# A hybrid encoder layer on one core: fewer, larger transfers for bias, reciprocals and v, and the modulation's gate by columns

## The chip, the cores and the metric

The kernel runs on one core of a Trainium2 chip. Its time is device microseconds of one execution. Five engines work side by side: TensorE (PE) multiplies matrices, VectorE (DVE), ScalarE (ACT) and GpSimd (POOL) do elementwise work, and SyncE (SP) issues nearly all transfers between DRAM and on-chip memory. The transfers themselves run on the core's 16 DMA engines.

## The reference

A layer over 512 tokens of 1024 channels, in float32: a modulated norm, one wide projection, a recurrent branch (A), a windowed attention branch (B), and a gated merge.

```python
mod = silu(c) @ w_c + b_c                     # 3 * 1024 columns
shift, scl, gate = split(mod, 3)
h = rms_norm(x, g_pre) * (1 + scl) + shift
xa, za, q, k, v, zb, ga, gb = split(h @ w_in, 8)      # each 512 x 1024
xa  = depthwise_conv(xa)
y_a = (rg_lru(xa, forward) + rg_lru(xa, backward)) * silu(za) @ w_pa
y_b = neighbourhood_attention(q, k, v, rpb) * silu(zb) @ w_pb
merged = sigmoid(ga) * y_a + sigmoid(gb) * y_b
x = rms_norm(x + gate * (merged @ w_o), g_final)
```

The tokens are a grid of 8 rows and 64 columns. The attention has 16 heads of 64; each query sees all 8 rows and 16 columns around its own, and a bias table rpb is added to the scores.

## The kernel before

Each matrix product is made of three: operands are split into a high part (rounded to the engine's fp32r) and a low remainder, and high x high, high x low and low x high are added. So a weight tile wraw (128 x 1024, 512 KB) is loaded by SP, cast by ACT into whi, and subtracted by POOL or DVE into wlo; then 24 matmuls of 128 x 512 use it. That is one `proj`, a projection of 128 output channels for all tokens.

The stages, in the order of the program:

1. The head: x and the modulation's weights arrive; shift and scale are made as columns (one value to a partition) by a multiply-and-add over rows (`modulate`); h is made tile by tile, and with each tile of h TensorE adds to the eight tiles of v (`vmm`). There are dummy matmuls in the first microseconds (`fill`).
2. v leaves through `vout`: ACT and DVE split a tile of v (128 tokens x 512 channels) into va, and SP writes it to a scratch tensor in DRAM (vscr0 for the first four pairs of heads, vscr1 for the others), eight writes of 512 KB.
3. The attention works on four groups of two pairs of heads. For each pair there are three projections (q, k, z), numbered by `main` from 9 on: 9, 10, 11 for pair 0, 12, 13, 14 for pair 1. Then `scores` multiplies q and k for both pairs, and `attend` does softmax and the product with v, while TensorE goes on with the next group's projections between its pieces. The rows of v are reloaded from vscr by `load_v`, in column-major order of the grid, as pieces vt. `bias` loads the bias braw, and POOL makes the masked tables nb. The reciprocals of the softmax's sums go through a DVE transpose, a 16 KB write to rscr with the access pattern `turned` and a reload as rcx that repeats them over 64 partitions; DVE then multiplies z's gate sz by rcx.
4. The recurrent branch, its gates, and the products with w_pb.
5. The merge: projections with w_pa, and `gate_row`, which makes the modulation's gate as a row: 16 loads wr of w_c, 16 multiply-adds on DVE (g), a split, four matmuls with ones (mi) that repeat the row over partitions, and the bias on top.
6. The product with w_o, whose rows are multiplied by the gate first, and the final norm.

The order on every engine is set ahead by a planner (`Plan`): an operation has a rank, dependencies and an estimated cost, and is placed on its engine when the estimate lets it begin. Large tiles come from NW slots of 128 x 1024, small ones from NS slots of 128 x 512. The engines then run their lists in order, and wait for what a row needs. SP's transfers take turns on eight counters (DMAHW0 to DMAHW7): a transfer waits until the one eight before it has landed.

A load's access patterns are written outermost dimension first. These are the ones of the transfers that the change and the prediction name, in the program before:

```python
src = bass.AP(rpb.tensor, ..., [[RPB_C, ROWS], [1, 16], [1, 256]])               # braw: 8 x 16 x 256 in DRAM
src = vscr[n].ap[g].rearrange("(r c) n -> c r n", r=ROWS)[c0:c0 + n // 8]        # vt: 16 (or 8) x 8 x 512
dst = vscr[n].ap[:, t * P:(t + 1) * P, :].rearrange("g p c -> p g c")            # vscr: 128 x 2 x 512
return bass.AP(scr.tensor, scr.offset, [[32, 4], [P, 32], [1, 32]])              # rscr: 4 x 32 x 32
src = bass.AP(scr.ap.tensor, ..., [[0, 64], [2 * P, 4], [1, P]])                 # rcx: 64 x 4 x 128, twice
```

The on-chip side is 128 partitions, 64 for rcx and for the half pieces of vt.

Of the kernel before, what the change touches and what calls it, by code (L numbers as in the profile page):

```python
# [8 lines left out]
F32 = mybir.dt.float32  # L9
# [20 lines left out]
NS, NW = 36, 32  # L30
# [3 lines left out]
QP, QE, BD = 1, 1, 0  # L34
LIMITS = {"hx": 8, "acc": 3, "sp": 8, "pt": 2, "pv": 2, "mi": 2, "hd": 3, "gt": 8}
# [297 lines left out]
def layer(ctx, tc, x, x_t, par, w_m, w_g, bc_gate, w_v, w_in, w_blk, rpb, amask, w_pa, w_pb, w_o, g_final, out):  # L333
# [64 lines left out]
    ident, onesc, onesr = const("ident", [P, P]), const("onesc", [P, P]), const("onesr", [P, P], F32R)  # L398
    prm, silc, msk, par_sb = const("prm", [P, 120]), const("silc", [P, KD]), const("msk", [P, 80]), const("par_sb", [120, P])
# [13 lines left out]
    op("PE", 0.25, lambda e: nc.tensor.transpose(pp0.ap[:, :120], par_sb.ap, ident.ap[:120, :120]), -20,  # L413
       r=[par_sb, ident], w=[pp0])
    op("DVE", 0.3, lambda e: nc.vector.tensor_copy(prm.ap, pp0.ap[:, :120]), -20, r=[pp0], w=[prm])
# [14 lines left out]
    for n in range(2):  # L430
        cb = B("hx")

        def f(e, n=n, cb=cb):
            for k in range(4):
                nc.tensor.matmul(cb.ap[:, k * P:(k + 1) * P], ident.ap[:120, 4 * n + k:4 * n + k + 1].to_broadcast([120, P]), par_sb.ap,
                                 start=True, stop=True)
# [96 lines left out]
    def modulate(k):  # L533

        for m, d in ((1, scs), (0, shs)):
# [24 lines left out]
            load(t, whole(t), w_m[2 * k + m], k - 5, 524288, spare=2, name=f"wc{k}{m}")  # L560
# [103 lines left out]
    vscr = [pl.fixed(dp.tile([2, S, 512], F32, name=f"vscr{n}")) for n in range(2)]  # L664

    def vout(u, rank):
        n, t = u
        a = W("va", F32R)

        def view(off, step):  # L670
            part = list(a.ap.ap)[0]
            return bass.AP(a.ap.tensor, a.ap.offset + off, [part, [256, 4], [step, 2], [1, 64]])
        src = lambda: vps[u].ap.rearrange("p (a b c) -> p a b c", a=4, b=2)
        op("ACT", act(512), lambda e: nc.scalar.copy(view(0, 192), src()), rank, r=[vps[u]], w=[a], name="voh")
        op("DVE", dve(512), lambda e: nc.vector.tensor_tensor(view(64, 64), src(), view(0, 192).bitcast(F32), op=ALU.subtract),
           rank, r=[vps[u]], rw=[a], name="vol")
        dst = vscr[n].ap[:, t * P:(t + 1) * P, :].rearrange("g p c -> p g c")
        op("SP", 0.6, lambda e: nc.sync.dma_start(dst, a.ap.bitcast(F32).rearrange("p (g c) -> p g c", g=2)), rank - 3,
           r=[a], w=[vscr[n]], size=524288, name="vout")
# [43 lines left out]
    def bias(pr, rank, after):  # L723
        raw = T("braw")
        rv = lambda: raw.ap.rearrange("p (h f) -> p h f", h=2)
        base = RPB_L - 1 - (PAD + 2 * pr * RPB_N + RPB_C * (ROWS - 1) + 7 + 255)
        for h in range(2):
            src = bass.AP(rpb.tensor, rpb.offset + base - h * RPB_N, [[RPB_C, ROWS], [1, 16], [1, 256]])
            load(raw, lambda h=h: rv()[:, h, :], src, rank - 4, 131072, after=after, spare=4, name="bias")
        res = []  # L730
        for v0, w, m0 in ((0, 32, 0), (8, 24, 32), (0, 24, 56)):
            nb = T("nb")
            res.append(nb)
            for h in range(2):
                def f(e, h=h, nb=nb, v0=v0, w=w, m0=m0):
                    part = list(raw.ap.ap)[0]
                    mv = msk.ap[:, m0:m0 + w].unsqueeze(1).to_broadcast([P, ROWS, w])
                    view = bass.AP(raw.ap.tensor, raw.ap.offset + h * 256 + 255 - v0, [part, [-RPB_C, ROWS], [-1, w]])
                    o = nb.ap.rearrange("p (h f) -> p h f", h=2)[:, h, :ROWS * w].rearrange("p (r c) -> p r c", c=w)
                    nc.gpsimd.tensor_tensor(o, mv, view, op=ALU.subtract)  # L740
                op("POOL", pool_(ROWS * w), f, rank - 1, r=[raw, msk], w=[nb], after=after, spare=2, name="nb")
        return res
# [7 lines left out]
    def load_v(g, after):  # L750
        for b in (0, 3, 1, 2):
            for j, (c0, r0) in enumerate(PIECES[b]):

                a = vt[g, b, j] = T("vt", F32R)
                n = 64 if (b, j) in ((0, 1), (3, 0)) else P
                src = vscr[g // 2].ap[g % 2].rearrange("(r c) n -> c r n", r=ROWS)[c0:c0 + n // 8]
                load(a, lambda a=a, r0=r0, n=n: a.ap[r0:r0 + n, :].bitcast(F32), src, 8 + 6 * g - 1.5 + 0.1 * (b > 0), n * 2048,
                     r=[vscr[g // 2]], after=after, spare=3, name="vt")
                if n == 64:
                    op("POOL", 0.7, lambda e, a=a, r0=r0: nc.gpsimd.memset(a.ap[64 - r0:P - r0, :].bitcast(F32), 0.0), 8 + 6 * g - 1.5,  # L760
                       w=[a], after=after, spare=3, name="vz")
# [42 lines left out]
    def attend(pr, sps, z, nbt, pos, pos0):  # L804
# [3 lines left out]
        def half(bs):  # L808
# [10 lines left out]
            for members in groups:  # L819
# [12 lines left out]
                for i, (b, h) in enumerate(members):  # L832
                    def f(e_, i=i, b=b, h=h, pv2=pv2):
                        c = 2 * bs.index(b) + h
                        nc.scalar.activation(pv2(i), pv2(i), AF.Exp, bias=mn.ap[:, c:c + 1], scale=-1.0,  # L835
                                             accum_out=sm.ap[:, 2 * b + h:2 * b + h + 1])
# [17 lines left out]
                def f(e_, members=members, ppv=ppv):  # L854
                    for i, (b, h) in enumerate(members):
                        e = bs.index(b)
                        for j in range(2):
                            mm(pv[h].ap[:, e * 256:(e + 1) * 256], vt[pr // 2, b, j].ap[:, off + h * P:off + (h + 1) * P],
                               ppv()[:, (i if edge else 2 * i) + j].rearrange("p s q -> p (s q)"), j == 0, j == 1)
                op("PE", 0.49, f, rk - 0.4, r=[pp] + [vt[pr // 2, b, j] for b in dict(members) for j in range(2)],  # L860
# [46 lines left out]
    def small(rank, after):  # L907
# [4 lines left out]
        op("DVE", 0.2, lambda e: nc.vector.tensor_scalar(silc.ap, pc(0, 8), 0.5, None, op0=ALU.mult), rank, r=[prm], w=[silc])  # L912
# [24 lines left out]
    for g in range(4):  # L937
        sets, zs, nbs = [], [], []
        for pr in (2 * g, 2 * g + 1):
            n0 = len(main)  # L940
            nbs.append(bias(pr, n0 + BD * (1 - pr % 2), gate_of(n0, 2) if pr else [main[6]]))
            if pr % 2 == 0:
                load_v(pr // 2, gate_of(n0, 2) if pr else [])
# [3 lines left out]
            sets.append(split(q, k))  # L947
        pos = k[0] + 0.6 + QP
        for i, sps in enumerate(scores(sets, pos, ends[-1:] if QE else [])):
            attend(2 * g + i, sps, zs[i], nbs[i], pos + 3 * i, pos)  # L950

# [141 lines left out]
    def gate_row(pos, after):  # L1093
        op("ACT", 0.3, lambda e: nc.scalar.copy(onesr.ap, onesc.ap), pos, r=[onesc], w=[onesr], after=after)
        g = (T("g"), T("g"))
        for kk in range(KD):
            for n in range(2):
                wr = T("wr")
                load(wr, whole(wr), w_g[kk * P:(kk + 1) * P, n * 512:(n + 1) * 512], pos + 0.5 * kk, 262144,
                     after=after, spare=12, name="wr")  # L1100

                def f(e, kk=kk, n=n, wr=wr):
                    if kk == 0:
                        nc.vector.tensor_scalar(g[n].ap, wr.ap, silc.ap[:, 0:1], None, op0=ALU.mult)
                    else:
                        nc.vector.scalar_tensor_tensor(g[n].ap, wr.ap, silc.ap[:, kk:kk + 1], g[n].ap, op0=ALU.mult, op1=ALU.add)
                op("DVE", dve(512), f, pos + 3 + 0.5 * kk, r=[wr, silc], **({"rw": [g[n]]} if kk else {"w": [g[n]]}), lock=True,
                   name="grow")
        for n in range(2):
            gh, gl = T("gh", F32R), T("gl", F32R)  # L1110
            op("ACT", act(512), cast(whole(gh), whole(g[n])), pos + 8, r=[g[n]], w=[gh])
            op("DVE", dve(512), sub(whole(gl), whole(g[n]), whole(gh)), pos + 8, r=[g[n], gh], w=[gl], lock=True)
            o, bcg, gf = B("mi"), T("gate"), T("gfin")

            def f(e, gh=gh, gl=gl, o=o):
                mm(o.ap, onesr.ap, gh.ap, True, False)
                mm(o.ap, onesr.ap, gl.ap, False, True)
            op("PE", 0.46, f, pos + 8, r=[onesr, gh, gl], w=[o], name="grow")
            load(bcg, whole(bcg), bc_gate[n * 512:(n + 1) * 512].partition_broadcast(P), pos + 7, 262144, after=after, spare=8)

            def f(e, o=o, bcg=bcg):
                nc.vector.tensor_tensor(bcg.ap, o.ap, bcg.ap, op=ALU.add)

                nc.vector.tensor_scalar(bcg.ap, bcg.ap, 0.5, None, op0=ALU.mult)
            op("DVE", dve(512) + dve2(512), f, pos + 8.2, r=[o], rw=[bcg], lock=True, name="gate")
# [203 lines left out]
```

## Time and profile before

| | |
|---|---|
| median of 3 runs | 561.11 us (560.77 to 564.41) |
| profiled execution, its own time | 561.85 us |
| its span, first to last instruction | 560.1 us |
| granted TensorE clock | 0.996 |
| TensorE busy | 550.8 us |
| DVE, ACT, POOL busy | 392.7, 322.1, 99.0 us |
| moved by DMA | 83.58 MB, 36509 packets |

The page gives busy times by engine, then 40 slices of the span, the DMA queues, the chain of work that ended last, the costliest groups of instructions and the transfers. Queue q1 is SP's, q10 ACT's. A row of a timeline has the start and the duration in us; a row of a group has busy time, the mean of one in ns, and the idle time ahead of it with what ended it. A row of windows begins with the stretch, then has busy time for PE, PEld, DVE, ACT and POOL, the granted clock, the mean busy share of the 16 DMA engines, and GB/s.

### The profile page before, as it was taken

The page shows a single profiled execution, that of the slowest core. Times are in us where ns is not written, and L with a number is a line of the kernel's source. Part 1 is how long each engine was busy: PE and PEld are TensorE (multiplying, and loading weights), DVE is VectorE, ACT ScalarE, POOL GpSimd, SP SyncE. Part 2 cuts the span into 40 slices and gives each one's busy share as a digit, 9 for nine tenths or more (in the row PEclk, how much of TensorE's full clock was granted, in tenths as well). Part 3 has the DMA queues.
Part 4 walks back from the last instruction along what each step waited for, and adds up shares of the span by engine and source line. Part 5 has one row for each costly group of instructions (what it writes and reads, how often), then busy time and mean ns, then how long its engine had stood idle before and what let it go on. Part 6 is the DMA issues. An engine that isn't in the chain of part 4 may idle for free.

```text
span 560.1 us, 7705 instructions
## 1 busy us (share of the span) xinstructions
PE 550.8 (98%) x2773; PEld 458.0 (82%) x2773; DVE 392.7 (70%) x712; ACT 322.1 (58%) x560; POOL 99.0 (18%) x97
## 2 busy tenths in 40 slices
PE   8999999999999999999999999999999999999995
PEld 8888888788888888887887888888788888888885
DVE  5998723684884886897569648866967897469523
ACT  6542523862763763777965984995698243223243
POOL 1102539453553540000000000000000000000220
PEclk9999999999999999999999999999999999999998
DMA  8993899439249244034333134032319452380002
GB/s 302 409 407 109 308 272 286 128 109 235 66 120 248 59 135 149 2 97 151 112 113 95 39 112 142 28 114 75 114 59 361 144 188 75 130 321 1 0 39 113
DMA packets 36509, 83.58 MB, mean 149 GB/s; under 512 B 4607, under 2 KB 11895, under 8 KB 36471
## 3 DMA queue, kind: packets, MB, share of 16 engines
q1 hardware_dynamic: 36192, 82.76, 45.2%
q8 instruction: 22, 0.36, 0.3%
q10 hardware_dynamic: 279, 0.32, 0.2%
q14 instruction: 16, 0.13, 0.1%
HBM read 76.65 MB, written 6.42 MB: 148 GB/s over the span
## 4 chain that ended last, share of the span: by engine, by line
PE 96%; DMA 2%; DVE 0%; SPq 0%; ACT 0%; POOL 0%; issue 0%; POOLq 0%
PE acc L384 78%; PE hx L384 8%; PE pv L384 3%; PE pt L842 2%; PE gt L384 2%; PE sp L384 2%; DMA wv<-in_w_v_dram 1%; DMA xT<-in_x_t_dram 1%; SPq L373 0%; POOL vl L381 0%; PE mi L384 0%; DVE yo L1216 0%; ACT vh L378 0%; DVE pp L850 0%; ACT pp L848 0%
## 5 line engine op out<-in xcount | busy, mean ns | idle before, releaser
L384 PE MATMUL acc<-hhl,whi 128*128 128x512 f32 x784 | 244.7, 393 | 0.0
L384 PEld LDWEIGHTS acc<-hhl,whi 128*128 128x128 f32 x784 | 143.7, 188 | 27.6 <-issue 0.4
L384 PE MATMUL acc<-hhl,wlo 128*128 128x512 f32 x392 | 152.9, 390 | 0.0
L384 PEld LDWEIGHTS acc<-hhl,wlo 128*128 128x128 f32 x392 | 73.6, 188 | 15.8
L378 ACT CAST whi<-wraw 128x1024 fp32r<-128x1024 f32 x72 | 74.2, 1044 | 9.1 <-DMA wraw<-in_w_in_dram 8.5
L1195 POOL TENSOR_TENSOR yo<-yo,gfin 128x512 f32<-128x512 f32 x6 | 8.0, 1339 | 338.0 <-ACT xr L1192 337.9
L381 POOL TENSOR_TENSOR wlo<-wraw,whi 128x1024 fp32r<-128x1024 f32 x23 | 56.1, 2444 | 63.6 <-ACT whi L378 49.4
L381 DVE TENSOR_TENSOR wlo<-wraw,whi 128x1024 fp32r<-128x1024 f32 x49 | 59.4, 1220 | 8.2 <-ACT whi L378 8.0
L384 PE MATMUL acc<-woh,mhl 128*128 128x512 f32 (+1 forms) x144 | 40.4, 365 | 0.0
L384 PE MATMUL acc<-yahl,whi 128*128 128x512 f32 x128 | 39.4, 389 | 0.0
L384 PE MATMUL acc<-ybhl,whi 128*128 128x512 f32 x128 | 39.4, 389 | 0.0
L740 POOL TENSOR_TENSOR nb<-msk,braw 128x192 f32<-128x192 f32 (+1 forms) x48 | 27.7, 610 | 35.6 <-DMA braw<-in_rpb_dram 29.4
L835 ACT ACTIVATE p<-p,mn 128x192 f32<-128x192 f32 (+1 forms) x64 | 30.5, 478 | 5.9 <-DVE mn L828 5.8
L384 PE MATMUL hx<-vh,hhl 128*128 128x512 f32 x112 | 33.5, 389 | 0.0
L828 DVE CUSTOM_DVE_ANT_0 p<-sp,nb 128x192 f32<-128x192 f32 (+1 forms) x64 | 31.6, 608 | 0.9 <-PE sp L384 0.7
L1070 DVE SCALAR_TENSOR_TENSOR gm<-gm,acc 128x512 f32<-128x512 f32 x16 | 11.0, 687 | 28.6 <-PE acc L384 28.5
L384 PEld LDWEIGHTS acc<-woh,mhl 128*128 128x128 f32 x144 | 26.1, 189 | 4.4
L384 PEld LDWEIGHTS acc<-yahl,whi 128*128 128x128 f32 x128 | 24.0, 188 | 5.0
L384 PEld LDWEIGHTS acc<-ybhl,whi 128*128 128x128 f32 x128 | 24.0, 188 | 5.0
L976 DVE SCALAR_TENSOR_TENSOR xc<-acc,prm,xc 128x511 f32<-128x511 f32 (+1 forms) x24 | 18.0, 749 | 12.3 <-ACT xc L969 11.7
L850 DVE TENSOR_TENSOR pp<-pt,pp 128x384 fp32r<-128x384 f32 (+1 forms) x32 | 19.5, 625 | 10.1 <-ACT pp L848 9.8
L384 PE MATMUL acc<-wol,mhl 128*128 128x512 f32 (+1 forms) x72 | 26.3, 365 | 0.0
(202 smaller groups left out, 960.7 us busy)
## 6 DMA issues: line engine op xcount, KB each, us to landing
wraw<-in_w_in_dram SPq DMA_DIRECT2D x56, 512.0 KB, 5.6
wc<-in_w_m_dram SPq DMA_DIRECT2D x14, 512.0 KB, 9.1
vt<-vscr SPq DMA_DIRECT2D x24, 256.0 KB, 7.8
vscr<-va SPq DMA_DIRECT2D x8, 512.0 KB, 5.3
wraw<-in_w_pb_dram SPq DMA_DIRECT2D x8, 512.0 KB
wraw<-in_w_pa_dram SPq DMA_DIRECT2D x8, 512.0 KB, 7.6
wr<-in_w_g_dram SPq DMA_DIRECT2D x16, 256.0 KB, 3.9
wo<-in_w_o_dram SPq DMA_DIRECT2D x8, 512.0 KB, 3.7
```

Source lines behind the costliest of these rows:

```text
L378: return lambda e: nc.scalar.copy(o(), i()) if e == "ACT" else nc.vector.tensor_copy(o(), i())
L381: return lambda e: ENGINE[e].tensor_tensor(o(), a(), b().bitcast(F32), op=ALU.subtract)
L384: nc.tensor.matmul(o, a, b, start=first, stop=last)
L740: nc.gpsimd.tensor_tensor(o, mv, view, op=ALU.subtract)
L828: nc.vector.tensor_tensor_reduce(out=o, in0=v(spv(h, e)[:, :nk]), in1=v(nb[:, h, :nk]), scale=1.0, scalar=3e38, op0=ALU.add, op1=ALU.min, ...
L835: nc.scalar.activation(pv2(i), pv2(i), AF.Exp, bias=mn.ap[:, c:c + 1], scale=-1.0, accum_out=sm.ap[:, 2 * b + h:2 * b + h + 1])
L842: nc.tensor.transpose(ptp.ap[:, j * P:(j + 1) * P], pt_.ap[:, j * P:(j + 1) * P], ident.ap)
L850: op("DVE", dve(nt * P), lambda e_, ppv=ppv, pv4=pv4: nc.vector.tensor_tensor(ppv()[:, :, 1, :], pv4(), ppv()[:, :, 0, :].bitcast(F32), op ...
L976: nc.vector.scalar_tensor_tensor(a, b, wcol, a, op0=ALU.mult, op1=ALU.add)
L1070: op("DVE", dve(512), lambda e: nc.vector.scalar_tensor_tensor(t.ap, t.ap, 1.0, o.ap, op0=ALU.add, op1=ALU.mult), n - 1.9, r=[o], rw=[t], ...
L1195: op(("DVE", "POOL"), (dve(w), pool_(w)), lambda e: ENGINE[e].tensor_tensor(y(), y(), gfin[n].ap[:, gs], op=ALU.mult), rank + 0.1, r=[gfin ...
```

## The change

- **v out:** the scratch tensor has rows of 1024 channels in column-major order of the grid (column, then row). A tile of 128 tokens is two grid rows of 64 columns, so the DRAM side of a write is 2 x 64 x 1024, rows of 4 KB.
- **v in:** `load_v` makes five transfers of eight: two of 512 KB that fill a large tile with two pieces, one of 256 KB and two of 128 KB. One piece is shared by two blocks. They read consecutive rows.
- **bias:** the host lays out a 128 x 512 table for each pair; one transfer of 256 KB instead of two.
- **reciprocals:** the sums are ordered by head, and one transfer of 256 KB repeats them for both, its DRAM side 2 x 64 x 512.
- **gate:** the weights are read as in `modulate`, eight loads wc of 512 KB among the weights of projections 23 to 30, each with one multiply-and-add on DVE into a column of gcol; then a transpose, a 16 KB write to gscr, and two reloads that repeat the row over 128 partitions. The 16 loads wr, DVE's 16 multiply-adds, the split, the four matmuls and the separate bias are gone. The parameter table par has 128 rows instead of 120.
- Slots: NS 36 to 34, NW 32 to 33.

```diff
-NS, NW = 36, 32
+NS, NW = 34, 33
+GR = 23
+VP, VG = 4, 3
-    vscr = [pl.fixed(dp.tile([2, S, 512], F32, name=f"vscr{n}")) for n in range(2)]
+    vscr = [pl.fixed(dp.tile([S, D], F32, name=f"vscr{n}")) for n in range(2)]
-        dst = vscr[n].ap[:, t * P:(t + 1) * P, :].rearrange("g p c -> p g c")
-        op("SP", 0.6, lambda e: nc.sync.dma_start(dst, a.ap.bitcast(F32).rearrange("p (g c) -> p g c", g=2)), rank - 3,
+        dst = vscr[n].ap.rearrange("(c r) n -> r c n", r=ROWS)[2 * t:2 * t + 2]
+        op("SP", 0.6, lambda e: nc.sync.dma_start(dst, a.ap.bitcast(F32)), rank - 3,
            r=[a], w=[vscr[n]], size=524288, name="vout")
-        for h in range(2):
-            src = bass.AP(rpb.tensor, rpb.offset + base - h * RPB_N, [[RPB_C, ROWS], [1, 16], [1, 256]])
-            load(raw, lambda h=h: rv()[:, h, :], src, rank - 4, 131072, after=after, spare=4, name="bias")
+        load(raw, whole(raw), rpb[pr], rank - 4, 262144, after=after, spare=4, name="bias")
-        for b in (0, 3, 1, 2):
-            for j, (c0, r0) in enumerate(PIECES[b]):
-                a = vt[g, b, j] = T("vt", F32R)
...
+        for (b0, j0), (b1, j1) in (((0, 0), (3, 1)), ((1, 0), (1, 1))):
+            a = W("vt", F32R)
+            src = bass.AP(src.tensor, src.offset, [[D, P], [D * ROWS * (c1 - c0), 2], [1, 512]])
+            load(a, lambda a=a: a.ap.rearrange("p (j n) -> p j n", j=2).bitcast(F32), src, pos + 0.1 * b1, 524288, **kw)
...
+        vt[g, 2, 0] = vt[g, 1, 1]
+        for b, j in ((0, 1), (3, 0), (2, 1)):
...
-        for h in range(2):
-            src = bass.AP(scr.ap.tensor, scr.ap.offset + h * P, [[0, 64], [2 * P, 4], [1, P]])
-            load(rcx, lambda h=h: rcx.ap[H[h], :].rearrange("p (b q) -> p b q", b=4), src, pos - 3, 131072, r=[scr], name="rcl", late=1.0)
+        src = bass.AP(scr.ap.tensor, scr.ap.offset, [[512, 2], [0, 64], [1, 512]])
+        load(rcx, whole(rcx), src, pos - 3, 262144, r=[scr], name="rcl", late=1.0)
+    for k in range(KD):
+        t, r = W("wc"), gcol.part()
+        load(t, whole(t), w_m[3 * k + 2], GR + k, 524288, after=[main[GR + k - 2]], spare=6, name=f"wc{k}2")
+        op("DVE", dve(1024) + 0.08, lambda e, k=k, t=t: nc.vector.tensor_tensor_reduce(
+            out=t.ap, in0=t.ap, in1=silr.ap, scale=0.5, scalar=pc(120 + k, 121 + k), op0=ALU.mult, op1=ALU.add,
+            accum_out=gcol.ap[:, k:k + 1]), GR + 3 + k, r=[silr, prm], rw=[t], w=[r], lock=True, name="gate")
+    op("DVE", 0.35, turn, GR + 12, rw=[gcol], w=[gtur], name="gturn")
+    op("SP", 0.5, lambda e: nc.sync.dma_start(turned(gscr.ap), gtur.ap[:, :32]), GR + 12, ...)
-        op("ACT", 0.3, lambda e: nc.scalar.copy(onesr.ap, onesc.ap), pos, r=[onesc], w=[onesr], after=after)
-        ...                                # gate_row: the 16 loads wr, g, gh and gl, the matmuls into mi, the bias
+            load(bcg, whole(bcg), bass.AP(gscr.ap.tensor, gscr.ap.offset + n * 512, [[0, P], [1, 512]]), pos + 7, 262144, r=[gscr],
+                 after=after, spare=8)
```

SP's list at the end of the head, before: the loads of projections 11 and 12 (wraw), the eight writes of v (vscr <- va), the loads of projections 13 and 14, and the first piece of v. In brackets stands what SP waits for ahead of a row.

```order
L373 DMA wraw_575<-in_w_in_dram 128x1024 [waits DMAHW1_49,DVE_49]
L373 DMA wraw_611<-in_w_in_dram 128x1024 [waits DMAHW2_49,DVE_49]
L678 DMA vscr_87<-va_620 128x2x512 [waits DMAHW3_49,DVE_49]
L678 DMA vscr_87<-va_627 128x2x512 [waits DMAHW4_49,DVE_49]
L678 DMA vscr_87<-va_633 128x2x512 [waits DMAHW5_49,DVE_49]
L678 DMA vscr_87<-va_640 128x2x512 [waits DMAHW6_49,DVE_49]
L678 DMA vscr_88<-va_647 128x2x512 [waits DMAHW7_49,DVE_49]
L678 DMA vscr_88<-va_655 128x2x512 [waits DMAHW0_49,DVE_49]
L678 DMA vscr_88<-va_664 128x2x512 [waits DMAHW1_49,DVE_49]
L678 DMA vscr_88<-va_673 128x2x512 [waits DMAHW2_49,DVE_49]
L373 DMA wraw_700<-in_w_in_dram 128x1024 [waits DMAHW3_49]
L373 DMA wraw_706<-in_w_in_dram 128x1024 [waits DMAHW4_49,PE_49]
```

The same place of SP's list after the change:

```order
L375 DMA wraw_606<-in_w_in_dram 128x1024 [waits DMAHW1_49,DVE_49]
L681 DMA vscr_85<-va_615 2x64x1024 [waits DMAHW2_49,DVE_49]
L681 DMA vscr_85<-va_622 2x64x1024 [waits DMAHW3_49,DVE_49]
L681 DMA vscr_85<-va_628 2x64x1024 [waits DMAHW4_49,DVE_49]
L681 DMA vscr_85<-va_635 2x64x1024 [waits DMAHW5_49,DVE_49]
L681 DMA vscr_86<-va_642 2x64x1024 [waits DMAHW6_49,DVE_49]
L681 DMA vscr_86<-va_650 2x64x1024 [waits DMAHW7_49,DVE_49]
L681 DMA vscr_86<-va_659 2x64x1024 [waits DMAHW0_49,DVE_49]
L681 DMA vscr_86<-va_668 2x64x1024 [waits DMAHW1_49,DVE_49]
L375 DMA wraw_695<-in_w_in_dram 128x1024 [waits DMAHW2_49]
L375 DMA wraw_701<-in_w_in_dram 128x1024 [waits DMAHW3_49,PE_49]
L375 DMA braw_730<-in_rpb_dram 128x512 [waits DMAHW4_49]
```

The writes stand at the same place, with 2 x 64 x 1024 for 128 x 2 x 512; the load of projection 13 (the first wraw behind them) waits for the counter of the first write, as before, and one bias load now stands ahead of the pieces of v.

SP's list at the reciprocals of the first group, before:

```order
L894 DMA rscr_91<-rct_1171 4x32x32 [waits DMAHW2_49,DVE_49]
L373 DMA wraw_1222<-in_w_in_dram 128x1024 [waits DMAHW3_49]
L373 DMA rcx_1256<-rscr_91 64x4x128 [waits DMAHW4_49,DMAHW2_49]
L373 DMA rcx_1256<-rscr_91 64x4x128 [waits DMAHW5_49]
L894 DMA rscr_92<-rct_1291 4x32x32 [waits DMAHW6_49,DVE_49]
```

And after:

```order
L903 DMA rscr_89<-rct_1155 4x32x32 [waits DMAHW0_49,DVE_49]
L375 DMA wraw_1206<-in_w_in_dram 128x1024 [waits DMAHW1_49]
L375 DMA rcx_1265<-rscr_89 128x1x512 [waits DMAHW0_49,DMAHW2_49,PE_49,Activation_49]
L903 DMA rscr_90<-rct_1277 4x32x32 [waits DMAHW3_49,DVE_49]
L375 DMA wraw_1304<-in_w_in_dram 128x1024 [waits DMAHW4_49]
```

Two loads of 64 partitions became one of 128, whose row shows the on-chip side; its place between the writes of the reciprocals and the weight loads is the same.

More of the change, by code (lines that the diff above doesn't have):

```diff
@@ L332, in layer @@
 @with_exitstack
-def layer(ctx, tc, x, x_t, par, w_m, w_g, bc_gate, w_v, w_in, w_blk, rpb, amask, w_pa, w_pb, w_o, g_final, out):
+def layer(ctx, tc, x, x_t, par, w_m, w_v, w_in, w_blk, rpb, amask, w_pa, w_pb, w_o, g_final, out):
     nc = tc.nc
@@ L396, in const @@
         return pl.fixed(cp.tile(shape, dt, name=name))
-    ident, onesc, onesr = const("ident", [P, P]), const("onesc", [P, P]), const("onesr", [P, P], F32R)
-    prm, silc, msk, par_sb = const("prm", [P, 120]), const("silc", [P, KD]), const("msk", [P, 80]), const("par_sb", [120, P])
+    ident, onesc = const("ident", [P, P]), const("onesc", [P, P])
+    prm, msk, par_sb = const("prm", [P, P]), const("msk", [P, 80]), const("par_sb", [P, P])
     tan8 = const("tan8", [8, P])
@@ L412, in layer @@
     pp0 = B("mi")
-    op("PE", 0.25, lambda e: nc.tensor.transpose(pp0.ap[:, :120], par_sb.ap, ident.ap[:120, :120]), -20,
+    op("PE", 0.25, lambda e: nc.tensor.transpose(pp0.ap[:, :P], par_sb.ap, ident.ap), -20,
        r=[par_sb, ident], w=[pp0])
-    op("DVE", 0.3, lambda e: nc.vector.tensor_copy(prm.ap, pp0.ap[:, :120]), -20, r=[pp0], w=[prm])
+    op("DVE", 0.3, lambda e: nc.vector.tensor_copy(prm.ap, pp0.ap[:, :P]), -20, r=[pp0], w=[prm])
     pc = lambda a, b: prm.ap[:, a:b]
@@ L434, in f @@
             for k in range(4):
[L435 removed]
+                nc.tensor.matmul(cb.ap[:, k * P:(k + 1) * P], ident.ap[:, 4 * n + k:4 * n + k + 1].to_broadcast([P, P]), par_sb.ap,
                                  start=True, stop=True)
@@ L1093, in gate_row @@
     def gate_row(pos, after):
-        op("ACT", 0.3, lambda e: nc.scalar.copy(onesr.ap, onesc.ap), pos, r=[onesc], w=[onesr], after=after)
[L1095 to L1108, printed above, removed]
-        for n in range(2):
[L1110 to L1125, printed above, removed]
+        for n in range(2):
+            bcg, gf = T("gate"), T("gfin")
+            load(bcg, whole(bcg), bass.AP(gscr.ap.tensor, gscr.ap.offset + n * 512, [[0, P], [1, 512]]), pos + 7, 262144, r=[gscr],
+                 after=after, spare=8)
             gate.append(bcg)
```

61 lines of the change are left out of this document (36 added, 25 removed).

## The prediction

> **What bounds the kernel now.** I read the busy table first, then the chain of waits, then the table of who waited for whom.
>
> ```profile
> PE 550.8 (98%) x2773; PEld 458.0 (82%) x2773; DVE 392.7 (70%) x712; ACT 322.1 (58%) x560; POOL 99.0 (18%) x97
> PE 96%; DMA 2%; DVE 0%; SPq 0%; ACT 0%; POOL 0%; issue 0%; POOLq 0%
> PE hx L502 <- POOL epsc L450: 1.5, 1, 1.5
> PE pv L384 <- DVE pp L850: 1.1, 1, 1.1
> PE hx L384 <- POOL vl L381: 0.2, 1, 0.2
> ```
>
> TensorE is the bound: 550.8 of 560.1 us, and behind the head it waited once, 1.1 us in the first attention. So a change that only relieves DVE, ACT, POOL or the queue can win at most that 1.1 us and the matmuls it deletes. What it can lose is open: everything TensorE multiplies arrives by SP's one queue. The chain around the v writes:
>
> ```profile
> 54.98 5.44 PE hx L384 x24
> 60.42 32.64 PE acc L384 x144
> 93.06 2.98 PE sp L384 x48
> 82.01 0.39 PE L384 MATMUL acc<-hh,whi 128*128 128x512 f32 x1
> 57.03 8.47 SPq L678 DMA_DIRECT2D vscr<-va  x8
> 65.55 2.56 SPq L373 DMA_DIRECT2D wraw<-in_w_in_dram  x2
> ```
>
> The 144 matmuls from 60.42 are six projections of 5.44 us, numbers 9 to 14 of the program. Number 13 starts at 82.01 (each starts with hh,whi). Its weights are the first of the two wraw loads issued right behind the eight vscr writes.
>
> **How many DMA engines a transfer gets.** This decides the case, so it is worked out from four kinds of rows.
>
> ```profile
> q10 hardware_dynamic: 279, 0.32, 0.2%
> DMA packets 36509, 83.58 MB, mean 149 GB/s; under 512 B 4607, under 2 KB 11895, under 8 KB 36471
> wraw<-in_w_in_dram SPq DMA_DIRECT2D x56, 512.0 KB, 5.6
> ...
> braw<-in_rpb_dram SPq DMA_DIRECT2D x16, 128.0 KB
> vt<-vscr SPq DMA_DIRECT2D x8, 128.0 KB
> out_dram<-yo ACTq DMA_DIRECT2D x1, 256.0 KB
> rscr<-rct SPq DMA_DIRECT2D x8, 16.0 KB
> par_sb<-in_par_dram ACTq DMA_DIRECT2D x1, 60.0 KB
> msk<-in_amask_dram SPq DMA_DIRECT2D x1, 40.0 KB
> 109.95:110.10 0.15, 0.15 (x3) 0.11 (x2) 0.15 (x1) 0.07 (x1) 0.15 (x1) 1.00 0.35 55
> 98.11 1.31 SPq L373 DMA_DIRECT2D braw<-in_rpb_dram  x2
> 99.40:101.00 1.60, 1.31 (x6) 0.75 (x4) 0.00 (x0) 1.24 (x2) 0.12 (x1) 1.00 0.51 104
> ```
>
> ACT's queue (q10) made two transfers: par_sb of 120 rows and an output of 128 rows. 279 packets are 248 rows and 31 more, which is 16 + 15: one closing packet for each engine used, sixteen for 128 rows, fifteen for 120. The 25 rows of issues, from which these are taken, add up to 234 transfers. Of the 4607 small packets 1024 are the rscr rows (8 x 128 of 128 bytes) and 128 the mask's; 3455 are left. Sixteen for each of 234 would be 3744. The 289 that are missing are exactly those of the transfers whose outer dimension on one side is no multiple of 16: braw (8 outside) 16 x 8, the half vt (8) 8 x 8, rscr (4 on the DRAM side) 8 x 12, par 1. So a transfer runs on as many engines as the outer dimension allows. The windows (their last two columns are DMA share and GB/s) fit: while an rscr write moves alone, the share is 0.35, though its 128 rows could keep all engines busy (four engines are 0.25; I put the rest down to records of so short packets that overlap). And while the two braw loads of 98.11 are in flight together, it stays at a half: the second doesn't take the other eight engines.
>
> The new vscr write has the DRAM side 2 x 64 x 1024: the same form as rscr, with a 2 where that has a 4. I take **two engines**, and by the braw pair the same two for all eight writes.
>
> [...]
>
> **The v writes, step by step.**
>
> ```profile
> 36.40:39.60 3.20, 3.20 (x15) 2.65 (x15) 3.20 (x5) 1.05 (x3) 0.00 (x0) 1.00 1.03 409
> 58.00:68.00 10.00, 10.00 (x46) 8.29 (x45) 7.22 (x14) 6.66 (x10) 6.37 (x6) 1.00 1.03 379
> wv<-in_w_v_dram SPq DMA_DIRECT2D x7, 512.0 KB, 10.2
> wo<-in_w_o_dram SPq DMA_DIRECT2D x8, 512.0 KB, 3.7
> L378 ACT CAST whi<-wraw 128x1024 fp32r<-128x1024 f32 x72 | 74.2, 1044 | 9.1 <-DMA wraw<-in_w_in_dram 8.5 <-PE acc L384 0.4
> L381 POOL TENSOR_TENSOR wlo<-wraw,whi 128x1024 fp32r<-128x1024 f32 x23 | 56.1, 2444 | 63.6 <-ACT whi L378 49.4 <-DVE hhl L598 7.3 <-DMA wraw<-in_w_in_dram 5.0
> L740 POOL TENSOR_TENSOR nb<-msk,braw 128x192 f32<-128x192 f32 (+1 forms) x48 | 27.7, 610 | 35.6 <-DMA braw<-in_rpb_dram 29.4 <-PE sp L384 6.1
> ```
>
> All engines full give 409 GB/s with 4 KB rows, 25.6 per engine; the writes now, of 2 KB rows, 379, 23.7 per engine, from 58.0 on. After the change the rows are 4 KB, so I take 25.6. Eight writes are 4.194 MB, 2.097 MB per engine: 81.9 us, done at 139.9. The queue serves in order: a wv load took 10.2 us to land with eight in flight (8 x 512 KB at 409 GB/s is 10.3), a wo load without a crowd 3.7. So the weights of projection 13 lie, with a sixteenth on each of the two engines, behind all eight writes, though they are issued as soon as the first is done: 32 KB more are 1.3 us, and 1.2 us until the landing is seen (half of wo's 3.7 less 1.3). At 142.4 ACT casts (1.04) and POOL subtracts (2.44), with 0.2 between: TensorE gets its third matmul of projection 13 at 146.1 instead of 82: **+64**.
>
> Queued behind meanwhile: SP with everything later (loads may have eight in flight, so vt and the next wraw go out as the writes end), ACT behind the cast, with the eviction of projection 11, POOL behind its subtraction. After 140 the backlog on the two engines is about 270 KB each, 10.6 us, so the weights of 15 to 17 are in by 152, and projections 13 and 14 keep TensorE busy until 157: nothing more. POOL has six bias subtractions of 0.61 before the weights of 14, 3.7 us, and 2.44: 152 against 151.5. Nothing again.
>
> By the lower rate, 23.7, the stall is 6.6 us longer. That two engines alone run faster than in a crowd has no row; the bound I take is the crowd's 25.6 with a fifth more, 13 us shorter.
>
> **The clock of a rested TensorE.**
>
> ```profile
> 1.51 3.35 PE L502 MATMUL hx<-onesc 128*128 128x128 f32 x14 [1.51 <-POOL epsc L450]
> 7.41 2.62 PE L502 MATMUL hx<-onesc 128*128 128x128 f32 x22
> ```
>
> The first 14 fillers took 239 ns each, the 22 later ones 119. If a pause of 64 us puts TensorE back there, some 3.4 us run at half speed: +1.7. It may be nothing, or 3; I take 1.5.
>
> **The other edits.** The reciprocals' rcx is one transfer with 2 outside on the DRAM side instead of two with 64: 131 KB per engine, 5.1 us.
>
> ```profile
> 110.64 1.31 SPq L373 DMA_DIRECT2D rcx<-rscr  x2
> rcx<-rscr SPq DMA_DIRECT2D x16, 128.0 KB, 3.7
> 119.31 0.69 DVE L898 TENSOR_TENSOR sz<-sz,rcx 128x512 f32<-128x512 f32 x1
> ```
>
> It lands up to 3.7 + 5.1 = 8.8 us behind its issue, and DVE multiplies with it 8.7 us behind (110.64 to 119.31). Where it is late DVE stands, and with it the pp that TensorE waits for: between nothing and 1 us, eight times. I take **+2** in all, 0 to 8 for the range. Weights that follow it have two projections of room.
>
> Deleted are four matmuls of the gate's broadcast, two pieces of 0.46 us: **-0.9**, the only work that leaves TensorE. DVE loses 14 x 0.745 + 2 x 0.48 us where TensorE waits for nobody, and gets 8 x (1.34 + 0.08) = 11.4 us in attention.
>
> ```profile
> 470.08 0.46 PE mi L384 x2
> L1106 DVE SCALAR_TENSOR_TENSOR g<-wr,silc,g 128x512 f32<-128x512 f32 x14 | 9.9, 745 | 0.0
> L569 DVE CUSTOM_DVE_ANT_0 wc<-wc,silr,mods 128x1024 f32<-128x1024 f32 x6 | 8.0, 1340 | 0.0
> 168.00:180.66 12.66, 12.66 (x58) 10.21 (x56) 5.67 (x9) 4.06 (x6) 5.32 (x3) 1.00 1.00 251
> 180.66:211.50 30.84, 30.84 (x200) 26.57 (x200) 24.51 (x66) 20.96 (x56) 14.01 (x15) 1.00 0.40 113
> ```
>
> DVE's idle time there is 7.0 us between two groups and 6.3 us in one, so the eight fit: 0, up to 4 if two or three of them stand ahead of an eviction. Bias and vt loads in fewer, larger pieces, the gate's column through a transpose (0.21 us, as the reciprocals' one) and its way through DRAM are covered by slack of tens of microseconds: 0. par with 128 rows: 0.
>
> **Sum**, against the profiled execution's own 561.85 (0.74 above the median of the runs shown): 561.85 + 64 + 1.5 + 2 - 0.9 = **628 us**.
>
> **Rivals.** *The writes spread after all* (chance 0.10): the pair of engines changes from write to write, or the 2 is folded away. Then 4 KB rows at 409 GB/s end at 68.3, projection 13 finds its weights, and 0.9 goes, with the 1.1 us wait at best: 560 us, no change. For it speaks that no row names the engines, and that the braw pair is one case; against it the exact 289 and that pair's half share. [...]
>
> *The queue lets later loads pass* (0.05): then projection 13 runs in time, and the wait is at the first pv: the four writes of vscr0 end at 99, their vt land some 8 us later (7.8 us now for 256 KB), against pv at 101.8: +5, 567 us. Against it: the 10.2 us of wv.
>
> *Everything as forecast* has 0.85. Its own range: 13 less for a faster pair, 6.6 more for a slower, 0 to 8 for rcx, 0 to 3 for the clock, 0 to 4 for DVE: 612 to 648. It holds about 0.8 in all, so the others stay outside it.
>
> One per cent, 5.6 us, is about what a measurement of this kernel can tell from no change. Faster by more needs matmuls that the change doesn't delete: 0.01. Within it: the first rival and half of the second, 0.12. Slower: 0.87.
>
> **What would show it.** Right: one wait of some 64 us on TensorE from 82, put down to wlo or the wraw load; DMA share near 0.13 and 50 GB/s from 70 to 138; vscr writes that land 10 to 80 us behind their issue; closing packets 332 fewer than sixteen for each transfer (8 x 14 for vscr, 8 x 14 for rcx, 9 x 12 for the transposed writes); the attention's rows as before, later by 65. Wrong: a share near 1 from 58 to 68 puts me in the first rival. A second wait at pv, or DVE idle before sz by rcx for over 1 us each, would mean that I undersized what comes behind.

## The result, and the profile after

The changed kernel takes **626.83 us** (median of 6 runs, 626.09 to 627.81), the kernel before 562.35 us (median of its 6 runs beside them, 560.77 to 564.41): ratio **1.114**, 95% interval 1.111 to 1.117. The change makes the kernel 11% slower; the forecast was 628 us.

The page of the changed kernel, its busy table and slices of 15.6 us each:

```profile
span 625.2 us, 7614 instructions
...
PE 553.6 (89%) x2769; PEld 458.8 (73%) x2769; DVE 389.4 (62%) x707; ACT 321.2 (51%) x557; POOL 106.1 (17%) x98
...
PEclk9999975557999999999999999999999999999999
DMA  8990111158335466452234322231231613173002
GB/s 314 408 376 10 54 52 53 53 185 291 129 112 169 160 206 216 161 169 81 73 109 142 101 85 84 88 116 48 91 132 45 225 67 102 52 258 127 1 34 102
DMA packets 29384, 82.53 MB, mean 132 GB/s; under 512 B 4132, under 2 KB 5284, under 8 KB 29348
```

TensorE's busy time is as before (553.6 against 550.8), its share has dropped from 98% to 89%: of the 65 us some 62 are idle time, nearly all of it in one piece. In slices 5 to 8 (62 to 125 us) the DMA engines are busy for a tenth, at 52 to 54 GB/s. The waits of TensorE, then the places:

```profile
PE acc L386 <- ACT whi L380: 60.6, 1, 60.6
PE pv L386 <- DVE pp L859: 1.7, 2, 1.1
...
PE acc L386 <- POOL wlo L383: 1.3, 1, 1.3
```

The timeline (start, duration, engine, instruction, in brackets the idle time before it) from the end of projection 12 to the restart:

```profile
81.92 0.39 PE L386 MATMUL acc<-hhl,wlo 128*128 128x512 f32 x1
141.77 1.04 ACT L380 CAST whi<-wraw 128x1024 fp32r<-128x1024 f32 x1 [69.71 <-DMA wraw<-in_w_in_dram]
142.86 0.80 PE L386 MATMUL acc<-hh,whi 128*128 128x512 f32 x1 [60.56 <-ACT whi L380]
142.94 2.36 POOL L383 TENSOR_TENSOR wlo<-wraw,whi 128x1024 fp32r<-128x1024 f32 x1 [74.80 <-ACT whi L380]
145.35 0.80 PE L386 MATMUL acc<-hh,wlo 128*128 128x512 f32 x1 [1.27 <-POOL wlo L383]
```

TensorE waits for the cast of projection 13's weights, and the cast waits for their load. SyncE's queue, which carries both the v writes and that load:

```profile
57.16 53.62 SPq L681 DMA_DIRECT2D vscr<-va  x8
110.84 17.78 SPq L375 DMA_DIRECT2D wraw<-in_w_in_dram  x2
128.67 1.20 SPq L375 DMA_DIRECT2D braw<-in_rpb_dram  x1
129.92 10.95 SPq L375 DMA_DIRECT2D vt<-vscr  x5
```

and the windows (the last three columns are granted clock, DMA share and GB/s):

```profile
70.00:80.00 10.00, 10.00 (x46) 8.29 (x45) 3.07 (x15) 0.60 (x1) 0.00 (x0) 1.00 0.13 53
110.00:120.00 10.00, 0.00 (x0) 0.00 (x0) 0.00 (x0) 0.00 (x0) 0.00 (x0) 0.50 0.13 52
130.00:140.00 10.00, 0.00 (x0) 0.00 (x0) 0.00 (x0) 0.00 (x0) 0.00 (x0) 0.50 0.63 214
```

A share of 0.13 is two of sixteen engines; 53 GB/s on two are 26.5 GB/s each. From 58 to 128 us nothing but the v writes moves (0.13 and 51 GB/s over the 70 us). SyncE stands on the issue of projection 13's load (16.69 of the 17.78 us of the two loads), and no other engine carries anything of it (the share stays at 0.13, with 53 GB/s) until that issue ends. From 128 to 136 us the share is 0.84 to 0.94 in stretches of 2 us: the other engines carry the loads, while the two still have writes ahead of them. From 138 to 141 us it is back at 0.13, with 52 GB/s: by the order of the queue, the loads' shares on the two engines, behind the writes. Then the cast can begin, at 141.77.

### The profile page after: what moved, and what is told of

Read it like the earlier page. It is cut to its first block, busy times and chain, and to the rows that moved or that the text cites. A ratio compares the mean times of both kernels' runs of the same rounds, so it can differ in the third digit from the quotient of the medians.

```text
span 625.2 us, 7614 instructions
## 1 busy us (share of the span) xinstructions
PE 553.6 (89%) x2769; PEld 458.8 (73%) x2769; DVE 389.4 (62%) x707; ACT 321.2 (51%) x557; POOL 106.1 (17%) x98
## 2 busy tenths in 40 slices
DMA packets 29384, 82.53 MB, mean 132 GB/s; under 512 B 4132, under 2 KB 5284, under 8 KB 29348
## 4 chain that ended last, share of the span: by engine, by line
PE 57%; DVE 0%; ACT 0%; issue 0%
PE acc L386 53%; PE gt L386 2%; PE pv L386 1%; PE pt L851 1%; PE sp L386 0%; DVE yo L1211 0%; DVE pp L859 0%; DVE yo L1179 0%; DVE xr L1183 0%; DVE p L837 0%; ACT sd L1201 0%; DVE q L1206 0%; DVE r L1203 0%; DVE rs L1207 0%; DVE ssq L1183 0%
## 5 line engine op out<-in xcount | busy, mean ns | idle before, releaser
L383 POOL TENSOR_TENSOR wlo<-wraw,whi 128x1024 fp32r<-128x1024 f32 x23 | 58.0, 2530 | 125.7 <-ACT whi L380 91.4
L386 PE MATMUL acc<-hh,whi 128*128 128x512 f32 x56 | 23.2, 414 | 60.6 <-ACT whi L380 60.6
L386 PEld LDWEIGHTS acc<-hh,whi 128*128 128x128 f32 x56 | 10.6, 189 | 64.8 <-ACT whi L380 61.0
L891 DVE SCALAR_TENSOR_TENSOR sz<-sz,acc 128x512 f32<-128x512 f32 x8 | 5.5, 683 | 81.7 <-ACT sz L890 81.7
L739 POOL TENSOR_TENSOR nb<-msk,braw 128x192 f32<-128x192 f32 (+1 forms) x48 | 32.6, 713 | 30.5 <-DMA braw<-in_rpb_dram 30.5
```

What stands on the lines that cost most here:

```text
L383: return lambda e: ENGINE[e].tensor_tensor(o(), a(), b().bitcast(F32), op=ALU.subtract)
L386: nc.tensor.matmul(o, a, b, start=first, stop=last)
L891: op("DVE", dve(512), lambda e: nc.vector.scalar_tensor_tensor(sz.ap, sz.ap, 1.0, oz.ap, op0=ALU.add, op1=ALU.mult), nz - 1.9, r=[oz], rw= ...
```

## Experiments

The order of the instructions is that of the changed kernel except for what the edit says; only where the queue's order is changed did the planner move rows on ScalarE, VectorE and GpSimd too. The edits are shown shortened, without their surroundings. The kernel before takes 561.4 to 562.0 us in the runs beside them.

**The writes cut by rows.** The DRAM side is then 64 x 1024 instead of 2 x 64 x 1024; layout, bytes and everything else stay.

```
-dst = vscr[n].ap.rearrange("(c r) n -> r c n", r=ROWS)[2*t:2*t+2]
-dma_start(dst, a.ap)
+dst = vscr[n].ap.rearrange("(c r) n -> r c n", r=ROWS)
+for j in range(2):
+    dma_start(dst[2*t + j], a.ap[64*j:64*j + 64, :])
```

> The changed kernel with each v write cut into two, one for each grid row: 64 rows of 4 KB, the same rows at the same addresses, sixteen writes of 256 KB whose outermost dimension is 64 on both sides. Nothing else differs, on any engine. Theory (an outermost dimension of 2 confines a write to two DMA engines): all sixteen engines work, the writes end by about 69 us, projection 13 waits for nothing, and the time is 562 us (the changed kernel's 626.8 less the 65 by which its first scores come later). Rival (rows of 4 KB that lie 32 KB apart in DRAM are slow to write, whatever the engines): the layout is the same, so it stays near 627 us.

Measured: **561.92 us** (561.38 to 562.46, 12 runs), ratio to the kernel before 0.9998 (0.9983 to 1.0013). SyncE's queue:

```profile
57.30 14.81 SPq L684 DMA_DIRECT2D vscr<-va  x16
72.16 1.64 SPq L375 DMA_DIRECT2D wraw<-in_w_in_dram  x2
```

and one window of it:

```profile
60.00:70.00 10.00, 10.00 (x46) 8.29 (x45) 6.97 (x18) 5.15 (x7) 5.79 (x4) 1.00 0.83 269
```

Twice as many transfers are issued in 14.8 us instead of 53.6, at a share of 0.83, and TensorE's 60.6 us are gone. The whole loss is the outer 2 of one access pattern. The new layout in DRAM, the larger bias and v loads, the reciprocals' load and the gate's columns together cost nothing that can be measured.

**The writes cut the other way**, by halves of the 1024 columns: each is then 2 x 64 x 512, as many transfers as in the kernel above, with the outer 2 left.

```
+for j in range(2):
+    dma_start(dst[:, :, 512*j:512*j + 512], a.ap[:, 512*j:512*j + 512])
```

> The changed kernel with each v write cut into two by channels: 2 x 64 x 512, so again sixteen writes of 256 KB, as many and as large as in the cut by grid rows, but the outermost dimension stays 2. Theory: still two engines, now with rows of 2 KB, which the kernel before moved at 23.7 GB/s per engine instead of 25.6: 88 us of writing, some 633 us, and a DMA share of 0.13 in the stall. Rival (size, number or order of the transfers matters, not the outermost dimension): like the cut by grid rows, 562 us.

Measured: 628.64 us (one run). All its writes together (SyncE's time to issue one, shortest, median and longest in ns, and first and last start):

```profile
L684 SPq DMA_DIRECT2D vscr<-va x16: 499/4954/7156, 56.8 to 123.3; - x16
```

and a window while they run:

```profile
100.00:110.00 10.00, 0.00 (x0) 0.00 (x0) 0.00 (x0) 0.00 (x0) 0.00 (x0) 0.50 0.13 51
```

It isn't the number of transfers, it is the 2. Rows of 2 KB cost 2 us here, not the 6 I had expected: 51 GB/s against 53, so on two engines the row's length matters less than the 379 against 409 GB/s of all sixteen had said. Those two stretches differ in more than the rows, though: the 409 are loads alone. With rows of 4 KB on all sixteen engines the v writes moved 269 GB/s at a share of 0.83, in the window of the kernel above.

**Half the dose**: only the four writes of vscr0 are cut by rows.

```
+if n:
+    dma_start(dst[2*t:2*t + 2], a.ap); return
```

> The changed kernel where the four writes of vscr0 are cut by grid rows (64 outermost) and the four of vscr1 keep 2 x 64 x 1024. Theory: half of the bytes go through two engines, 41 us instead of 82, from about 64 on; projection 13 starts some 35 us earlier than in the changed kernel: 591 us. Rival (the wait is for vscr0 to be read back, or for something else than the queue in front of the weights): vscr0 is there early, so about 562 us, or unchanged at 627.

Measured: 594.83 us (one run), 32.9 above the kernel with all writes cut; with none cut it is 64.9. TensorE's waits:

```profile
PE acc L386 <- ACT whi L380: 27.9, 1, 27.9
...
PE acc L386 <- POOL wlo L383: 1.3, 1, 1.3
```

Half the bytes on two engines, half the loss. The time is 4 us above the one expected; I put that down to the first four writes, which take time ahead of the others on all engines, but it wasn't tried.

**The clock after the wait.** TensorE is kept busy with idle matmuls during the wait.

```
+if pr == 1:   # ahead of projection 13
+    for _ in range(500):
+        nc.tensor.matmul(mi[:, :128], onesc, onesc)
```

> The changed kernel with 500 dummy matmuls of 128 x 128 ahead of projection 13, 119 ns each, which fill TensorE's wait to about 142 us and end before the weights are there. Theory (a rested TensorE starts at half clock): projection 13 then runs at full clock, 2 us less than the changed kernel, 624.8 us. Rival (the slow matmuls behind the wait have another cause, late operands): no change, 626.8 us.

Measured: 673.55 us (673.29 to 673.79), ratio 1.198. The fillers overran the wait by 50 us: 265 of them leave 530 records in the next kernel's trace, so a filler is two instructions, and together they took 0.223 us (500 from 81.95 to 193.53), not the 0.119 that I had taken from one row of the head. The run still answers the question, since the clock was full when projection 13 began. Third matmul and first score behind it:

```profile
194.08 0.40 PE L386 MATMUL acc<-hh,wlo 128*128 128x512 f32 x1
204.64 0.36 PE L386 MATMUL sp<-kh,qh 64*128 64x192 f32 x2
```

That is 10.56 us; before it was 10.52 (82.47 to 92.99), and in the changed kernel 12.62 (145.35 to 157.97). So the rested clock costs 2.1 us. The same with 265 fillers, which end inside the wait:

> The changed kernel with 265 idle fp32 matmuls of 128x128 ahead of projection 13; e4's profile had 500 of them take 111.6 us (81.95 to 193.53), 0.223 us each, so 265 end near 141.1, just ahead of the weights' cast at 142.8. Theory (the clock of a rested TensorE costs about 2 us after the wait): no matmul of projection 13 is at 0.427 us, the granted clock is 1.00 to the end of the wait and after, and the time is 1.5 to 2.5 us below the changed kernel's 626.8: 624.3 to 625.3. Rival (the slow matmuls after the wait were hidden by something else that was late too, as wlo on GpSimd): 626.5 to 627. If the fillers run past 142.8 they add what they overrun.

Measured: 626.49 us (626.06 to 626.58, 4 runs), the rival's number. The restart:

```profile
137.74 4.52 PE L955 MATMUL mi<-onesc 128*128 128x128 f32 x39
143.60 0.50 PE L386 MATMUL acc<-hh,whi 128*128 128x512 f32 x1 [1.34 <-ACT whi L380]
146.10 0.80 PE L386 MATMUL acc<-hh,wlo 128*128 128x512 f32 x1 [1.77 <-POOL wlo L383]
```

and the clock there:

```profile
146.00:148.00 2.00, 1.90 (x5) 1.51 (x6) 0.27 (x1) 0.00 (x0) 2.00 (x5) 0.50 1.08 325
```

The clock was full until about 145.5 and at 0.50 from there to 148.9 (0.88 in the mean of 144 to 146, 0.77 of 148 to 150): it fell within the second of two gaps of 1.34 and 1.77 us, with two matmuls between them. Third matmul to first score: 11.98 us (146.10 to 158.08), 0.64 better than the changed kernel; the weights came 0.74 later in this run. So the fillers don't pay here, though the clock's 2.1 us are real.

**The queue's order.** The weights of 13 go out behind the first v write, those of 14 behind the fifth.

```
-load(raw, w, rank=n - 5, ...)
+load(raw, w, rank=2.0 if n in (13, 14) else n - 5, ...)
```

> The changed kernel with the loads of the weights of projections 13 and 14 put ahead of most of the v writes in SyncE's queue (13 behind the first write, 14 behind the fifth); the writes stay on two DMA engines. Theory (the 60.6 us are the place in the queue, and the writes hold whatever stands behind them): projection 13 starts at 82 with no wait, 14 may wait until its place in the queue comes, about 108, and the long wait moves to projection 15, whose weights now stand behind the writes: it started at 96 before and would start at 146, so the time is some 14 us under the changed kernel's, 613 (608 to 618). Rival (the weights are slow because they share the two engines or the DRAM with the writes, wherever they stand in the queue): projection 13 still waits for tens of us, 620 to 628.

Measured: 622.99 us (one run), 10 more than expected and in the rival's range; the trace has to decide. TensorE and ScalarE:

```profile
114.43 0.80 PE L386 MATMUL acc<-hh,whi 128*128 128x512 f32 x1 [26.37 <-ACT whi L380]
153.50 0.53 PE L386 MATMUL sp<-kh,qh 64*128 64x192 f32 x2 [28.15 <-ACT kh L783]
145.15 1.04 ACT L380 CAST whi<-wraw 128x1024 fp32r<-128x1024 f32 x1 [29.79 <-DMA wraw<-in_w_in_dram]
152.86 0.59 ACT L783 ACTIVATE kh<-acc 128x512 fp32r<-128x512 f32 x1
```

Projection 13 ran at 82 without a wait, beside the writes, and 14 waited until its place came: so it is the place in the queue, and the rival falls. But the second wait isn't at projection 15, it is at the scores ahead of it, from 125 on (153.50 less 28.15). Their kh comes from projection 13, whose matmuls ended at 88, and stands on ScalarE behind the casts of the weights 14 to 17; the last three of these wait for loads behind the v writes. I had counted what stands behind the writes on the queue and left out what stands behind a cast on ScalarE.

**The reciprocals.** In the changed kernel and in the first experiment VectorE waits for rcx; and TensorE's start times there, against the kernel before, lose 2.1 us between the second and the fourth group of heads. Here the load is cut to 64 partitions as well.

```
-src = AP(scr, [[512, 2], [0, 64], [1, 512]]); load(rcx, src)
+for h in range(2):
+    dma_start(rcx[64*h:64*h + 64], AP(scr + 512*h, [[0, 64], [1, 512]]))
```

> The changed kernel with each v write issued as two transfers of 64x1024 (as in e1) and each reciprocal load issued as two of 64 partitions. What is asked is the reciprocals' term: in e1 the multiplication by rcx still waited 7.2 us in all for its transfer (4 waits), and TensorE's start times ran from -1.3 us at the second group of heads to +0.8 us at the fourth, against the kernel before, which is +2.1 us. Theory (the late reciprocals held TensorE): the four waits go, the +2.1 us go, and the time is 1 to 2.5 us below e1's 561.9, so 559.4 to 561, ratio to the kernel before 0.995 to 0.998. Rival (VectorE's gate columns, or the smaller slack of the new order, cost the 2.1 us): the waits go, the time stays at 561.5 to 562.5. Second rival (each transfer to one row of 64 partitions still falls on few engines): the waits stay.

Measured: 562.16 us (561.57 to 563.74, 12 runs), ratio 1.0002 (0.9989 to 1.0014). The four waits for rcx, which were these in the first experiment, are gone:

```profile
DVE sz L909 <- DMA rcx<-rscr: 7.2, 4, 2.4
```

and the time has not moved, nor have the start times: they still lose 2.1 us there. The late reciprocals cost TensorE nothing. The rival's time, then; where do the 2.1 us come from? TensorE's only new waits in the first experiment are two at pv, and ahead of each VectorE spends long on a tiny instruction, the doubling of the row sums, whose end is that of GpSimd's subtract beside it:

```profile
154.40 0.75 PE L386 MATMUL pv<-pp,vt 128*128 128x256 f32 x4 [0.52 <-DVE pp L862]
198.11 0.74 PE L386 MATMUL pv<-pp,vt 128*128 128x256 f32 x4 [1.12 <-DVE pp L862]
194.17 1.97 DVE L898 TENSOR_SCALAR rc<-sm 128x8 f32<-128x8 f32 x1
193.72 2.39 POOL L383 TENSOR_TENSOR wlo<-wraw,whi 128x1024 fp32r<-128x1024 f32 x1 [5.71 <-issue]
```

In the kernel before, the same doubling meets the same subtract, but begins 0.1 us ahead of it and not 0.45 us behind:

```profile
194.07 0.17 DVE L886 TENSOR_SCALAR rc<-sm 128x8 f32<-128x8 f32 x1
194.17 2.40 POOL L381 TENSOR_TENSOR wlo<-wraw,whi 128x1024 fp32r<-128x1024 f32 x1 [6.01 <-ACT whi L378]
```

**The doubling beside GpSimd.** Three edits of that one instruction, on top of the writes cut by rows.

```
-nc.vector.tensor_scalar(rc[:, :8], sm, 2.0, op0=mult)
+for i in (slice(0, 7), slice(7, 8)):       # first;  second: (0, 4), (4, 8)
+    nc.vector.tensor_scalar(rc[:, i], sm[:, i], 2.0, op0=mult)
+nc.scalar.mul(rc[:, :8], sm, 2.0)          # third, alone
```

> e1 (v writes of 64 rows) with VectorE's doubling of the row sums (128x8) written as two instructions of 7 and of 1 columns. In e1 and in the changed kernel two of the eight doublings take 1.38 and 1.97 us instead of 0.17, and end with the subtract of GpSimd beside them (150.97+1.38=152.35 against 149.91+2.40=152.31; 194.17+1.97=196.14 against 193.72+2.39=196.11); behind them stand VectorE's subtracts that release pv, and TensorE waits 0.52 us at 154.40 and 1.12 us at 198.11. [...] Theory (GpSimd holds up the doubling, and an odd count frees it): all sixteen pieces take about 0.17 us, the two waits for pv go, and the time is 1 to 1.6 us below e1's: 560.3 to 561, ratio to the kernel before 0.997 to 0.998. Rival (the odd count makes no difference, or the next instruction, the reciprocal, is held in its place): pieces or reciprocals of over 1 us, the waits stay, 561.5 to 562.5.

> The same with 4 and 4 columns in place of 7 and 1: as many instructions, all of even counts. [...] Rival (it is enough that the doubling is cut in two or begins later): all pieces at 0.17 us.

Measured: 562.02 us (561.36 to 563.30, 12 runs; ratio 1.0008, 0.9995 to 1.0022) and 562.45 us (one run). In both the first piece is held at the same two places; with 7 and 1:

```profile
193.65 2.04 DVE L899 TENSOR_SCALAR rc<-sm 128x7 f32<-128x7 f32 x2
193.22 2.39 POOL L383 TENSOR_TENSOR wlo<-wraw,whi 128x1024 fp32r<-128x1024 f32 x1 [5.57 <-issue]
```

again to one end (195.69 and 195.61). At the other place the two pieces take 1.44 us; with 4 and 4 they take 1.45 and 2.03. So the number of columns, odd or even, makes no difference. The first of these runs had been expected to free the doubling, the second to leave it held and the time at the first experiment's 561.9 us. That an odd number would free it was a guess of mine, which no row had shown.

> e1 (v writes of 64 rows) with the doubling of the row sums (128x8) done by ScalarE, which writes them where VectorE's reciprocal reads them; all else in the same order. [...] Theory (the doubling, a one-source VectorE instruction from SBUF to SBUF, is what GpSimd's subtract holds up): ScalarE's doubling takes some 0.2 us at all eight places, the reciprocal 0.20 us, the two waits for pv (0.52 and 1.12 us) go, and the time is 1 to 1.6 us below e1's: 560.3 to 561. Rival (any VectorE instruction from SBUF to SBUF is held there): the reciprocal takes over 1 us at the two places in the doubling's stead, the waits stay, 561.5 to 562.5.

Measured: **561.00 us** (560.52 to 561.60, 12 runs), ratio 0.9987 (0.9972 to 1.0003).

```profile
194.46 2.41 POOL L383 TENSOR_TENSOR wlo<-wraw,whi 128x1024 fp32r<-128x1024 f32 x1 [5.95 <-issue]
194.91 0.20 DVE L899 RECIPROCAL rc<-rc 128x8 f32<-128x8 f32 x1
165.84 0.74 PE L386 MATMUL pv<-pp,vt 128*128 128x256 f32 x4 [1.05 <-DVE pp L862]
```

The reciprocal, in the doubling's place and beside the same subtract, takes 0.20 us; the waits of 0.52 and 1.12 us are gone, and one of 1.05 us has come at another pv. The theory holds for the instruction: it is the doubling on VectorE that GpSimd's subtract holds up, not every instruction of VectorE from SBUF to SBUF. The order of the two starts goes with it: begun 0.45 us behind the subtract the doubling took 1.97 us, begun 0.1 us ahead of it 0.17. Why the doubling is held there and the reciprocal is not, no row shows. As to the time, it is the lowest here, 0.9 us under the first experiment, and not told apart from the kernel before. TensorE's start times now lose 1.4 us between the second and the fourth group instead of 2.1; where the rest comes from stays open.

## Why the prediction was right

Point by point, by its terms:

- **Two engines for the v writes.** Right, and shown: a share of 0.13, and 64.9 us that go when the outer 2 goes and halve when half of it goes. The packets agree to one: the changed page's issues are 199 transfers; of 4132 small packets 1280 are the rscr, gscr and mask rows, and the 2852 left are 332 fewer than sixteen each, the number forecast. The cut kernels agree too: sixteen writes on sixteen engines would close with 240 packets more than eight on two, sixteen writes on two with 16 more, the half dose with 120 more, and the small packets went from 4132 to 4372, 4148 and 4252. That all eight writes share one pair follows from the constant 0.13, with some three writes outstanding.
- **The stall, +64.** Measured 62.9: third matmul at 145.35, forecast 146.1, before 82.47. The forecast had set its third matmul against the first one before, at 82.01, which makes the term 0.4 too large. The pair ran at 26.5 GB/s per engine instead of 25.6, and the cast began at 141.77 instead of 142.4. One detail was wrong and cost nothing: the writes were not all issued at once and then waited for in the engines. SyncE itself was held, for 9.35 us in the median write, so that some three were outstanding. The share of 0.13 therefore ended at 128 and not at 138, as the other engines carried loads while the pair still wrote; but the weights of 13 were complete only when the pair was through, as forecast.
- **Nothing more behind it.** Right: the backlog after 140 added no wait at the weights of 14 to 17.
- **The clock, +1.5.** Measured 2.1.
- **rcx, +2.** Wrong. DVE stood 9.0 us in four waits, the longest 3.1, where up to 1 us in each of eight had been forecast; waits of over 1 us had been named as the sign that the term was too small. TensorE lost nothing by them: the term was too large. What I took to follow, that a standing DVE delays the pp which TensorE waits for, failed: cutting the load took the waits away and left the time.
- **DVE and the gate's columns, 0 (up to 4).** Some 2.5 us were lost in attention between the second and the fourth group (start times 63.5 us late at the second, 66.0 at the fourth; 2.1 in the first experiment). Of these, 1.6 are the waits at pv behind the doubling: in the new order it begins behind GpSimd's subtract of the weights and not ahead of it. With the doubling on ScalarE only 0.7 of the first experiment's 2.1 went, since another wait came. It wasn't on my list; the second wait at pv had been named as a sign of a term too small, and was one. The columns themselves were not tried apart.
- **What went, -0.9.** The gate's matmuls: 0.95 between the last gate and the end. The wait of 1.1 us at the first pv also went (start times 65.0 late at the first group, 63.5 at the second); the sum had not counted that, and it takes back more than half of the row above.

Both rivals fell: the writes didn't spread, and projection 13's load didn't land ahead of them. The forecast's 66.6 us became 65.1 between the two spans: the stall 1.1 less, the clock 0.6 more, rcx 2 less, attention 2.5 more, the first pv 1.5 less. The large term was right for the right reason. That the small ones cancel was luck: rcx was charged 2 us that it didn't cost, and attention lost 2.5 in another way. The upper bound of 648 is 1.4 more than its own terms give (646.6); nothing hangs on that.

## What to carry to other kernels

Before merging transfers, look at the outermost dimension of the access pattern, here that of the DRAM side: a transfer with 2 outside used 2 of 16 DMA engines, and two transfers with 64 outside moved the same bytes 64.9 us sooner for the kernel. The transfer that was too narrow cost not its own consumer but what stood behind it on its queue, and, when two loads were moved ahead, what stood behind a waiting cast on ScalarE; follow both before saying what moving a load will gain. Here the closing packets and one window's DMA share of the kernel before told the number of engines ahead of any run of the change.

## What was not expected of the hardware

- SyncE's issue of a v write on the busy pair of engines took about as long as a transfer drained (512 KB at 53 GB/s are 9.9 us): 0.65 and 0.49 us for the first two, 9.35 in the median, 9.70 at most.
- On two engines 4 KB rows gave 26.5 GB/s per engine and 2 KB rows 25.5. On sixteen it was 25.6 in a stretch of loads with 4 KB rows and 23.7 in one with the v writes in 2 KB rows.
- The granted clock fell to 0.50 within two gaps of 1.34 and 1.77 us with two matmuls between them, and came back 2.8 us after steady work began again (146.1 to 148.9); after the 60 us wait that took 4.2 us (145.35 to 149.6).
- A doubling of 128x8 on VectorE took 1.97 us instead of 0.17 when it began 0.45 us behind the start of a GpSimd subtract, and 0.17 when it began 0.1 us ahead of it; a reciprocal at the same place behind that start took 0.20.
